# Entry of the feed-forward stage: small weight sums one column tile sooner, weight splits moved in VectorE's queue, output sums and the next splits inside the fixed order

## The chip, the core and the metric

The kernel runs on one core of a Trainium2 chip. A core has five engines with a queue each: TensorE (PE, matmuls; its weight loads are shown as PEld), VectorE (DVE), ScalarE (ACT), GpSimd (POOL), and SyncE (SP), which here only issues transfers. The metric is the device time of one execution in microseconds; lower is better.

## The reference, cut to what matters

The reference is one layer over 1024 tokens of width 1024, all in float32: a normed and modulated mixer (stick-breaking attention beside a gated convolution) with an output projection, and then a feed-forward part. The change lies where the second begins:

```python
x = x + g1 * (merged @ w_out[l])

h = rmsnorm(x, ln2_g[l]) * (1.0 + sc2) + sh2
f = (jax.nn.silu(h @ w_ffn_gate[l]) * (h @ w_ffn_up[l])) @ w_ffn_down[l]
x = x + g2 * f
```

`w_ffn_gate` and `w_ffn_up` have 2816 columns, which are 22 column tiles of 128.

## The kernel before

**Products.** Each float32 operand is cut into a high part (`whi` of a weight, `rh` or `big` of an activation), which ScalarE writes by a copy to a rounded format, and a low part (`wlo`, `rl`), which VectorE writes as the difference (lines 134 and 1031). A product `half_prod` (line 123, called through `prod`) multiplies 512 rows of one 128-column weight tile with 512 tokens: four row tiles, three matmuls each (lines 129, 130, 131: high by high, high by low, low by high), so 12 matmuls of 128x512 into one of eight PSUM banks (`bank()`, line 1018).

**Seven products for a pair of column tiles.** Gate and up are computed for column tile j and column tile j+11 together, from the four 512-row blocks a11, a12, a21, a22 of the two, with seven products instead of eight (a Strassen form). Products 1 and 2 take a11 and a12 as they are; products 6, 5, 7, 3 and 4 take s2, s1, s3, s4 and a22, where s1 to s4 are sums of the blocks that GpSimd makes ("small weight sums", lines 149 to 153 for j = 0, lines 1323 to 1326 later). On the other side stand sums of quarters of the normed activation. Five additions on VectorE then make the four outputs (lines 1299 to 1303 and 1332 to 1342). `strassen(j, e, src)` does this for gate (e = 0) and up (e = 1), eleven times over j.

**The entry.** While the output projection ends (16 products `wo_prod`, a loop over m for token half 0 and one for token half 1), the weights for products 1 and 2 of j = 0 and j = 1 are loaded and split (`pre_weights`), and the raw tiles of j = 0 for the sums are loaded at m = 4 and m = 5. `wo_end` adds the residual on VectorE (line 1069), squares it on ScalarE (1075), stores it, and adds the square to a running sum `acc` on GpSimd (1078); the last square of half 1 is added by VectorE (1181). `sum2` sums over partitions with eight one-column matmuls (1085), `rstd_of` makes the factor (120, 121), and `spread2` brings it to all partitions with eight small matmuls (1091). Then `norm2` (1096) scales the eight tiles of token half 1, and VectorE and ScalarE make the activation factors of products 3, 7, 5, 6 (factor pairs `rh[2]`, `rh[6]`, `rh[5]`, `rh[4]`) and last `rh[3]` for product 4. Between them TensorE runs the products 1 and 2 of gate and up of j = 0 and j = 1 (`pre_prod`), then p3, p7, p6, p5 of gate, q6 of up, p4 of gate, and then q5, q7, q3, q4 of up.

**What sets the order.** From line 1109 to `ends = in_order(i0)` (1285) the order on each engine is the order in which the code is written. `plan_split` allots the buffers of a split and puts it on a list; `split_next` takes the next one from that list and places its ScalarE copy and its VectorE subtraction at this place of the two queues. `whi` and `wlo` are rings of nine buffers each, refilled when TensorE has read them. After line 1285 a planner with a cost model orders the instructions; those of j = 0 on VectorE and ScalarE come behind the last ones of the fixed order (`late`). Buffers of closed pools are used again: a new tile waits for the readers of the tile that lay there. `raw` has four buffers, so each load of a weight tile on SP's queue waits for the split or the sum that last reads an older one. From j = 1 on the sums on GpSimd write the tiles `ws0` to `ws3`, which lie where a quarter of the normed activation (`xb[1][1]`) lay.

In the eight PSUM banks, products 1 and 2 of j = 1 (gate and up) hold four until the loop reaches j = 1. p3, p7 and p5 hold one each until the output additions of gate read them.

Of the kernel before, what the change touches and what calls it, by code (L numbers as in the profile page):

```python
# [8 lines left out]
F32 = mybir.dt.float32  # L9
# [7 lines left out]
P = 128  # L17
# [11 lines left out]
def block_kernel(tc, x, x_t, cols, ada_1, ada_2, ada_row, w_q, w_kv, w_v1, w_cg, w_a, w_b, w_o, w_g, w_u, w_d, out):  # L29
# [1128 lines left out]
    for m in range(KT):  # L1158
# [14 lines left out]
        if m >= 6:  # L1173
            spre.append(sums_in_place(*rsum[m - 6], *((wp.tile([P, 512], F32, name="s2"),) if m == 6 else ())))
# [24 lines left out]
    wq3 = plan_split(s4)  # L1199
# [3 lines left out]
    nc.scalar.activation(ca[0][1], p1, AF.Copy)  # L1203
    p2 = bank()
# [9 lines left out]
    for q in (2, 6, 3):  # L1214
        rh[q] = ep.tile([P, 4, 512], F32R, name=f"rh{q}")
        rl[q] = ep.tile([P, 4, 512], F32R, name=f"rl{q}")
# [4 lines left out]
    wq7 = plan_split(s3)  # L1221
# [18 lines left out]
    split_next()  # L1240
    p3 = bank()
    prod(p3, wq3, 2)
    wq6 = plan_split(s2)
# [8 lines left out]
    for j in range(4):  # L1252
        f_lo(5, j, xs(1, 1, j))
        nc.scalar.activation(rh[4][:, j], xs(0, 0, j), AF.Copy)
# [3 lines left out]
    wq5 = plan_split(s1)  # L1258
# [5 lines left out]
    s1, s2, s3, s4, au22 = spre[1]  # L1264
    s2 = xs(0, 0, 0)
    tt(nc.gpsimd, s2, au22, s3, ALU.subtract)
    tt(nc.gpsimd, s4, s4, s2, ALU.subtract)
    spre[1] = s1, s2, s3, s4, au22
    tt(nc.vector, c21, p6, c21, ALU.add)
    for j in range(4):  # L1270
        tt(nc.vector, xs(1, 0, j), xs(1, 0, j), xs(1, 1, j), ALU.subtract)
        nc.scalar.activation(rh[3][:, j], xs(1, 0, j), AF.Copy)
        if j == 1:
            uq6 = plan_split(s2)
            split_next()
# [6 lines left out]
    tt(nc.vector, ca[1][1], q6, ca[1][1], ALU.add)
    p4 = bank()
    prod(p4, wq4, 3)
    ends = in_order(i0)
    pre[0, 1] = ca[1]
# [284 lines left out]
```

## Time and profile before

| | us |
|---|---|
| median of three runs (lowest, highest) | 1885.09 (1882.09, 1885.92) |
| the profiled execution: its own time | 1887.14 |
| its span, from the first to the last instruction | 1885.0 |
| TensorE busy | 1818.8 (96%) |
| VectorE busy | 1340.6 (71%) |
| ScalarE busy | 777.4 (41%) |
| GpSimd busy | 413.6 (22%) |
| mean granted TensorE clock | 0.987 |

Rows of a timeline give start, duration, engine, line, operation, the tiles written and read, the shape, the count, and in brackets how long the engine had stood idle before, and what ended that. Durations of matmuls that follow each other overlap: a stream at full clock has 0.39 us a matmul, started 0.227 us apart. Rows of the stage view give a stretch, its length, the busy time (and instructions) of PE, PEld, DVE, ACT and POOL, the granted clock as a share of full speed, the transfers' share and rate.

### The profile page before, as it was taken

How to read it: one execution, taken by the hardware profiler on the slowest of the kernel's cores; microseconds unless marked ns; L12 is line 12 of the kernel's file. 1: busy time of each engine (PE TensorE's matmuls, PEld its weight loads, DVE VectorE, ACT ScalarE, POOL GpSimd, SP SyncE). 2: the span in 40 equal slices, each digit the busy share in tenths (PEclk: the TensorE clock that was granted, in tenths of full speed). 3: DMA queues.
4: the chain of work that ended last, by engine and by line, in shares of the span. 5: the costliest groups of instructions: out<-in, count | busy, mean ns of one | idle time of the engine just before them, and what ended most of it. 6: DMA issues, size and time to landing. Idle time of an engine off the chain costs nothing.

```text
span 1885.0 us, 24611 instructions
## 1 busy us (share of the span) xinstructions
PE 1818.8 (96%) x8765; PEld 1506.0 (80%) x8765; DVE 1340.6 (71%) x1896; ACT 777.4 (41%) x1462; POOL 413.6 (22%) x292
## 2 busy tenths in 40 slices
PE   7999999999999999979999999989999999999999
PEld 5787778887788988867888788877888888888787
DVE  6873877779854888867788544579987778743953
ACT  4342653332334656645556322344444344422220
POOL 1043338332420000000000001235554545300000
PEclk9999999999999999989999999998999999999999
DMA  9598452238538566677553534505444344289766
GB/s 389 199 305 302 162 173 79 73 104 303 207 123 254 149 189 180 167 223 219 158 161 101 182 129 167 174 27 169 152 174 155 134 145 169 111 341 320 253 233 214
DMA packets 154112, 351.94 MB, mean 187 GB/s; under 512 B 15211, under 2 KB 54397, under 8 KB 151814
## 3 DMA queue, kind: packets, MB, share of 16 engines
q1 hardware_dynamic: 96336, 239.54, 39.9%
q10 hardware_dynamic: 56646, 107.16, 15.6%
q0 software_dynamic: 1008, 3.67, 0.5%
q8 instruction: 70, 1.15, 0.3%
q14 instruction: 52, 0.43, 0.1%
HBM read 240.73 MB, written 109.58 MB: 186 GB/s over the span
## 4 chain that ended last, share of the span: by engine, by line
PE 78%; DVE 10%; DMA 7%; issue 2%; ACT 2%; POOL 1%; SPq 0%; ACTq 0%; DVEq 0%; POOLq 0%
PE e L129 7%; PE e L130 7%; PE e L131 7%; PE pj L129 5%; PE pj L130 5%; PE pj L131 5%; PE pj L292 5%; PE pj L851 4%; PE pj L852 4%; PE pj L853 4%; PE e L1414 3%; PE e L1412 3%; PE e L1413 3%; PE tr L784 3%; PE o L800 2%
## 5 line engine op out<-in xcount | busy, mean ns | idle before, releaser
L769 DVE TENSOR_TENSOR_SCAN pt<-pt,mk 128x128 f32<-128x128 f32 (+7 forms) x128 | 172.1, 1350 | 54.6 <-ACT pt L765 53.9
L134 POOL TENSOR_TENSOR acc<-acc,sq 128x512 f32<-128x512 f32 x13 | 16.8, 1291 | 650.8 <-ACT sq L1075 650.8
L765 ACT ACTIVATE pt<-z,rq 128x512 f32<-128x512 f32 (+1 forms) x192 | 107.7, 579 | 102.0 <-PE z L764 49.6
L129 PE MATMUL e<-big,whi 128*128 128x512 f32 x352 | 139.6, 396 | 5.5 <-DVE c L134 2.9
L134 DVE TENSOR_TENSOR wlo<-raw,whi 128x512 fp32r<-128x512 f32 x144 | 108.1, 761 | 45.7 <-ACT whi L468 33.5
L134 DVE TENSOR_TENSOR c<-e,c 128x512 f32<-128x512 f32 x154 | 103.2, 682 | 51.4 <-PE e L131 50.2
L130 PE MATMUL e<-big,whi 128*128 128x512 f32 x352 | 139.1, 395 | 0.0
L131 PE MATMUL e<-big,wlo 128*128 128x512 f32 x352 | 139.0, 395 | 0.0
L129 PE MATMUL pj<-big,whi 128*128 128x512 f32 x320 | 125.2, 391 | 5.0 <-ACT whi L468 2.6
L130 PE MATMUL pj<-big,whi 128*128 128x512 f32 x320 | 124.9, 390 | 0.0
L131 PE MATMUL pj<-big,wlo 128*128 128x512 f32 x320 | 124.5, 391 | 0.0
L1412 PE MATMUL e<-f,whi 128*128 128x512 f32 (+1 forms) x319 | 122.1, 383 | 1.3 <-ACT whi L1030 1.3
L1413 PE MATMUL e<-f,whi 128*128 128x512 f32 (+1 forms) x319 | 122.0, 383 | 0.0
L1414 PE MATMUL e<-f,wlo 128*128 128x512 f32 (+1 forms) x319 | 117.2, 384 | 3.3 <-DVE wlo L1031 3.3
L134 DVE TENSOR_TENSOR c<-pj,c 128x512 f32<-128x512 f32 x140 | 92.9, 682 | 34.0 <-PE pj L131 33.7
L134 POOL TENSOR_TENSOR ws<-raw,raw 128x512 f32<-128x512 f32 x40 | 56.9, 1422 | 267.6 <-DMA raw<-w_cg 123.2
L292 PE MATMUL pj<-whi,big 128*128 128x512 f32 x352 | 110.6, 401 | 2.9 <-ACT big L275 2.9
L468 ACT ACTIVATE whi<-raw 128x512 fp32r<-128x512 f32 x116 | 72.4, 628 | 95.4 <-PE pj L130 41.1
L788 DVE TENSOR_TENSOR atl<-tr,ath 128x512 fp32r<-128x512 f32 (+1 forms) x192 | 99.6, 549 | 12.3 <-ACT ath L787 10.7
L787 ACT ACTIVATE ath<-tr 128x512 fp32r<-128x512 f32 (+1 forms) x192 | 86.9, 489 | 48.0 <-PE o L799 29.6
L129 PE MATMUL e<-rh,whi 128*128 128x512 f32 x264 | 103.8, 393 | 2.9 <-DVE c L134 2.9
L851 PE MATMUL pj<-big,whi 128*128 128x512 f32 x256 | 105.0, 410 | 0.0
(255 smaller groups left out, 4992.3 us busy)
## 6 DMA issues: line engine op xcount, KB each, us to landing
f<-d_f SPq DMA_DIRECT2D x77, 512.0 KB, 4.3
d_f<-fs ACTq DMA_DIRECT2D x70, 512.0 KB, 2.7
raw<-w_cg SPq DMA_DIRECT2D x40, 512.0 KB, 3.6
raw<-w_g SPq DMA_DIRECT2D x24, 512.0 KB, 3.4
raw<-w_u SPq DMA_DIRECT2D x24, 512.0 KB, 3.3
ad<-ada ACTq DMA_DIRECT2D x19, 512.0 KB, 4.6
ada<-ada SPq DMA_DIRECT2D x8, 1024.0 KB, 10.3
d_t<-ts SPq DMA_DIRECT2D x16, 512.0 KB, 5.4
```

Of the source, the lines that this page charges most:

```text
L129: nc.tensor.matmul(ps, wh[:, k, :], fh[:, k, :], start=(k == 0), stop=False)
L130: nc.tensor.matmul(ps, wh[:, k, :], fl[:, k, :], start=False, stop=False)
L131: nc.tensor.matmul(ps, wl[:, k, :], fh[:, k, :], start=False, stop=(k == 3))
L134: eng.tensor_tensor(out=out, in0=a, in1=b, op=op)
L292: nc.tensor.matmul(ps, a, b, start=(k == 0 and q == 0), stop=(k == KT - 1 and q == 2))
L765: nc.scalar.activation(pt[:, off + s0:off + s0 + m], z[:, :m], AF.Sigmoid, scale=rq[:, 1, i, h:h + 1])
L769: nc.vector.tensor_tensor_scan(out=pt[:, rev], data0=pt[:, rev], data1=mk[:, rev], initial=1.0, op0=ALU.mult, op1=ALU.max)
L788: nc.vector.tensor_tensor(out=tl[:, :nb, c0:c0 + P], in0=src, in1=th[:, :nb, c0:c0 + P].bitcast(F32), op=ALU.subtract)
L851: nc.tensor.matmul(ps, wh, rh_, start=(k == 0), stop=False)
L1412: nc.tensor.matmul(o, wh, f[:, 0, c], start=(j == 0), stop=False)
L1413: nc.tensor.matmul(o, wh, f[:, 1, c], start=False, stop=False)
L1414: nc.tensor.matmul(o, wl, f[:, 0, c], start=False, stop=(j == NJ - 1))
```

## The change

It moves work in the fixed order. (1) GpSimd makes the sums of the gate's tiles at m = 5 instead of m = 6, and the first two of the up tiles' sums at m = 6 instead of m = 7; the other two (`t2`, and `t4` in place) come before the norm of token half 1 instead of after p5, in a tile of their own (`t2u`) instead of over `xs(0, 0, 0)`. (2) The splits are placed anew: wq7 directly after wq3, wq6 before the first `norm2`, wq5 after the first quarter of `rh[6]`, then uq6 (which fed q6), wq4, and uq5 one place each; uq7 stands among the output sums, uq3 and uq4 behind p4. All of them are in the fixed order; the four of up were the planner's before. (3) Four of the five output additions of gate, and with them the two output tiles `c12` and `c22`, come into the fixed order, ahead of the addition of q6 and of the request for p4's bank. (4) The buffers of `rh[3]`, `rl[3]` are opened after the last use of `t2u`. No operation is added or left out.

```diff
--- before.py
+++ after.py
@@ -1170,8 +1170,10 @@
         if 2 <= m < 6:
             split_next()
             split_next()
-        if m >= 6:
-            spre.append(sums_in_place(*rsum[m - 6], *((wp.tile([P, 512], F32, name="s2"),) if m == 6 else ())))
+        if m == 5:
+            spre.append(sums_in_place(*rsum[0], wp.tile([P, 512], F32, name="s2")))
+        elif m == 6:
+            spre.append(sums_in_place(*rsum[1]))
         ps = wo_prod(m, 1)
         if m == 0:
             r = sum2(0, (acc[0],))
@@ -1196,11 +1198,13 @@
 
     ca = [(ctile(f"c0{e}", cpa), ctile(f"c1{e}", cpa)) for e in range(2)]
     s1, s2, s3, s4, a22 = spre[0]
-    wq3 = plan_split(s4)
+    t1, t2, t3, t4, u22 = spre[1]
+    wq3, wq7 = plan_split(s4), plan_split(s3)
     p1 = pre_prod(0, 0)
     r = sum2(1, (acc[1],))
     split_next()
     nc.scalar.activation(ca[0][1], p1, AF.Copy)
+    split_next()
     p2 = bank()
     half_prod(p2, pw[0][1], rh[1], rl[1], 0, 3)
     rb1 = spread2(r)
@@ -1211,14 +1215,22 @@
     ep = s6.enter_context(tc.tile_pool(name="phe", bufs=1, reuse_waits="tile"))
     th, tl = big(), big()
     rh[4], rh[5], rl[4], rl[5] = th[:, 4:8], th[:, 0:4], tl[:, 4:8], tl[:, 0:4]
-    for q in (2, 6, 3):
-        rh[q] = ep.tile([P, 4, 512], F32R, name=f"rh{q}")
-        rl[q] = ep.tile([P, 4, 512], F32R, name=f"rl{q}")
+
+    def two(q):
+        rh[q], rl[q] = (ep.tile([P, 4, 512], F32R, name=f"r{t_}{q}") for t_ in "hl")
+
+    two(2)
+    two(6)
+    s2u = ExitStack()
+    t2 = s2u.enter_context(tc.tile_pool(name="phs2", bufs=1, reuse_waits="tile")).tile([P, 512], F32, name="t2u")
+    tt(nc.gpsimd, t2, u22, t3, ALU.subtract)
+    tt(nc.gpsimd, t4, t4, t2, ALU.subtract)
 
     def f_lo(q, j, src):
         tt(nc.vector, rl[q][:, j], src, rh[q][:, j].bitcast(F32), ALU.subtract)
 
-    wq7 = plan_split(s3)
+    wq6, wq5, uq6, wq4, uq5, uq7, uq3, uq4 = (plan_split(s) for s in (s2, s1, t2, a22, t1, t3, t4, u22))
+    split_next()
     for j in range(4):
         norm2(j, 1, rb1)
         tt(nc.gpsimd, xs(0, 0, j), xs(0, 1, j), xs(0, 0, j), ALU.subtract)
@@ -1237,10 +1249,10 @@
             op1=ALU.subtract)
         stt(out=xs(0, 1, j), in0=xs(1, 1, j), scalar=dsh2[:, j:j + 1], in1=xs(0, 1, j), op0=ALU.add, op1=ALU.subtract)
         nc.scalar.activation(rh[6][:, j], xs(0, 1, j), AF.Copy)
-    split_next()
+        if j == 0:
+            split_next()
     p3 = bank()
     prod(p3, wq3, 2)
-    wq6 = plan_split(s2)
     for j in range(4):
         stt(out=xs(1, 1, j), in0=xs(1, 1, j), scalar=mod[:, 2, 4 + j:5 + j], in1=xs(0, 0, j), op0=ALU.add,
             op1=ALU.subtract)
@@ -1250,61 +1262,59 @@
     prod(p7, wq7, 6)
     split_next()
     for j in range(4):
+        nc.scalar.activation(rh[4][:, j], xs(0, 0, j), AF.Copy)
         f_lo(5, j, xs(1, 1, j))
-        nc.scalar.activation(rh[4][:, j], xs(0, 0, j), AF.Copy)
     c11, c21 = ca[0]
     p6 = bank()
     prod(p6, wq6, 5)
-    wq5 = plan_split(s1)
     split_next()
     for j in range(4):
         f_lo(4, j, xs(0, 0, j))
     p5 = bank()
     prod(p5, wq5, 4)
-    s1, s2, s3, s4, au22 = spre[1]
-    s2 = xs(0, 0, 0)
-    tt(nc.gpsimd, s2, au22, s3, ALU.subtract)
-    tt(nc.gpsimd, s4, s4, s2, ALU.subtract)
-    spre[1] = s1, s2, s3, s4, au22
+    split_next()
+    s2u.close()
+    ep = s6.enter_context(tc.tile_pool(name="phe3", bufs=1, reuse_waits="tile"))
+    two(3)
     tt(nc.vector, c21, p6, c21, ALU.add)
     for j in range(4):
         tt(nc.vector, xs(1, 0, j), xs(1, 0, j), xs(1, 1, j), ALU.subtract)
         nc.scalar.activation(rh[3][:, j], xs(1, 0, j), AF.Copy)
-        if j == 1:
-            uq6 = plan_split(s2)
-            split_next()
     q6 = bank()
     prod(q6, uq6, 5)
-    wq4 = plan_split(a22)
-    split_next()
     for j in range(4):
         f_lo(3, j, xs(1, 0, j))
+    s5.close()
+    s7 = ExitStack()
+    cp = s7.enter_context(tc.tile_pool(name="phc2", bufs=1, side="right", reuse_waits="tile"))
+
+    def ct(tag, bufs):
+        return cp.tile([P, 512], F32, tag=tag, bufs=bufs, name=nm(tag))
+
+    c12, c22 = ct("c20", 1), ct("c30", 1)
+    tt(nc.vector, c12, p5, c21, ALU.add)
+    split_next()
+    tt(nc.vector, c22, p7, c12, ALU.add)
+    tt(nc.vector, c21, p7, c21, ALU.add)
+    tt(nc.vector, c12, p3, c12, ALU.add)
     tt(nc.vector, ca[1][1], q6, ca[1][1], ALU.add)
     p4 = bank()
     prod(p4, wq4, 3)
+    for _ in range(2):
+        split_next()
+    g00 = c11, c12, c21, c22
     ends = in_order(i0)
     pre[0, 1] = ca[1]
-    s5.close()
-    s7 = ExitStack()
-    cp = s7.enter_context(tc.tile_pool(name="phc2", bufs=1, side="right", reuse_waits="tile"))
-
-    def ct(tag, bufs):
-        return cp.tile([P, 512], F32, tag=tag, bufs=bufs, name=nm(tag))
 
     def strassen(j, e, src):
 
+        if (j, e) == (0, 0):
+            tt(nc.vector, g00[2], p4, g00[2], ALU.add)
+            return g00
         c12, c22 = ct(f"c2{e}", 1), ct(f"c3{e}", 1)
-        if (j, e) == (0, 0):
-            c11, c21 = ca[0]
-            tt(nc.vector, c12, p5, c21, ALU.add)
-            tt(nc.vector, c22, p7, c12, ALU.add)
-            tt(nc.vector, c21, p7, c21, ALU.add)
-            tt(nc.vector, c12, p3, c12, ALU.add)
-            tt(nc.vector, c21, p4, c21, ALU.add)
-            return c11, c12, c21, c22
         if (j, e) == (0, 1):
             c11, c21 = pre[j, e]
-            s1, s2, s3, s4, a22 = spre[1]
+            ws = dict(zip((5, 7, 3, 4), (uq5, uq7, uq3, uq4)))
         else:
             raw = load_raw(src[j])
             a11, a12 = raw[:, :512], raw[:, 512:]
@@ -1327,18 +1337,19 @@
             q6 = bank()
             prod(q6, split(s2), 5)
             tt(nc.vector, c21, q6, c21, ALU.add)
+            ws = {}
         q5 = bank()
-        prod(q5, split(s1), 4)
+        prod(q5, ws.get(5) or split(s1), 4)
         tt(nc.vector, c12, q5, c21, ALU.add)
         q7 = bank()
-        prod(q7, split(s3), 6)
+        prod(q7, ws.get(7) or split(s3), 6)
         tt(nc.vector, c22, q7, c12, ALU.add)
         tt(nc.vector, c21, q7, c21, ALU.add)
         q3 = bank()
-        prod(q3, split(s4), 2)
+        prod(q3, ws.get(3) or split(s4), 2)
         tt(nc.vector, c12, q3, c12, ALU.add)
         q4 = bank()
-        prod(q4, split(a22), 3)
+        prod(q4, ws.get(4) or split(a22), 3)
         tt(nc.vector, c21, q4, c21, ALU.add)
         return c11, c12, c21, c22
```

More of the change, by code (lines that the diff above doesn't have):

```diff
@@ L1272, in block_kernel @@
         nc.scalar.activation(rh[3][:, j], xs(1, 0, j), AF.Copy)
-        if j == 1:
-            uq6 = plan_split(s2)
-            split_next()
     q6 = bank()
     prod(q6, uq6, 5)
-    wq4 = plan_split(a22)
-    split_next()
     for j in range(4):
         f_lo(3, j, xs(1, 0, j))
[L1282 to L1286, printed above, removed]
     s5.close()
@@ L1292, in ct @@
         return cp.tile([P, 512], F32, tag=tag, bufs=bufs, name=nm(tag))
+    c12, c22 = ct("c20", 1), ct("c30", 1)
[4 more added lines that the diff above has]
+    tt(nc.vector, c12, p3, c12, ALU.add)
+    tt(nc.vector, ca[1][1], q6, ca[1][1], ALU.add)
+    p4 = bank()
+    prod(p4, wq4, 3)
+    for _ in range(2):
+        split_next()
+    g00 = c11, c12, c21, c22
+    ends = in_order(i0)
+    pre[0, 1] = ca[1]
     def strassen(j, e, src):
+        if (j, e) == (0, 0):
+            tt(nc.vector, g00[2], p4, g00[2], ALU.add)
+            return g00
         c12, c22 = ct(f"c2{e}", 1), ct(f"c3{e}", 1)
-        if (j, e) == (0, 0):
-            c11, c21 = ca[0]
-            tt(nc.vector, c12, p5, c21, ALU.add)
-            tt(nc.vector, c22, p7, c12, ALU.add)
-            tt(nc.vector, c21, p7, c21, ALU.add)
-            tt(nc.vector, c12, p3, c12, ALU.add)
-            tt(nc.vector, c21, p4, c21, ALU.add)
-            return c11, c12, c21, c22
         if (j, e) == (0, 1):
             c11, c21 = pre[j, e]
-            s1, s2, s3, s4, a22 = spre[1]
+            ws = dict(zip((5, 7, 3, 4), (uq5, uq7, uq3, uq4)))
         else:
```

## The prediction, made blind

> **What bounds the kernel now.** First the page, its chain of waits:
>
> ```profile
> PE 78%; DVE 10%; DMA 7%; issue 2%; ACT 2%; POOL 1%; SPq 0%; ACTq 0%; DVEq 0%; POOLq 0%
> ```
>
> TensorE's matmuls set the end, so a change pays where PE stands idle or runs slowly. Next PE's timeline through the entry, each stall with its neighbours:
>
> ```profile
> 1227.73 0.39 PE L131 MATMUL e<-big,wlo 128*128 128x512 f32 x1
> 1229.78 1.05 PE L1085 MATMUL e<-onec,acc 128*128 128x1 f32 x8 [1.66 <-DVE acc L134]
> ...
> 1233.42 1.91 PE L1091 MATMUL e<-dm,rs_r 128*128 128x128 f32 x8
> ...
> 1263.03 0.39 PE L131 MATMUL e<-big,wlo 128*128 128x512 f32 x1
> 1266.07 0.60 PE L129 MATMUL e<-big,whi 128*128 128x512 f32 x1 [2.65 <-ACT whi L1038]
> ...
> 1273.62 0.76 PE L129 MATMUL e<-rh,whi 128*128 128x512 f32 x1 [2.90 <-DVE c L134]
> ...
> 1280.87 0.76 PE L129 MATMUL e<-big,whi 128*128 128x512 f32 x1 [2.87 <-DVE c L134]
> ...
> 1287.14 0.40 PE L129 MATMUL e<-rh,whi 128*128 128x512 f32 x1
> ```
>
> Stall A (1.66 us) waits for the row sum; B (2.65), C (2.90) and D (2.87) stand before q6, p4 and q5. From 1263.26 (the last matmul of p5 plus 0.227) to 1287.14 PE does 39 matmuls: 12 of q6, 12 of p4, 15 of q5 and q7. At 0.227 each that is 8.84 us; it takes 23.88. So 15.0 are lost, 8.4 of them idle, the rest at a lower clock. Stages of 3.41 us show that:
>
> ```profile
> 1266.29:1269.70 3.41, 3.41 (x9) 2.43 (x9) 2.19 (x4) 2.30 (x4) 0.00 (x0) 0.50 0.00 0
> 1269.70:1273.11 3.41, 1.02 (x5) 0.50 (x3) 3.41 (x7) 3.40 (x7) 0.00 (x0) 0.99 0.45 154
> 1273.11:1276.53 3.42, 2.91 (x7) 2.37 (x8) 3.42 (x3) 0.56 (x2) 3.28 (x3) 0.51 0.00 0
> 1276.53:1279.94 3.41, 1.48 (x6) 0.86 (x5) 3.41 (x3) 1.67 (x3) 2.97 (x2) 1.00 0.16 26
> 1279.94:1283.35 3.41, 2.48 (x6) 2.02 (x7) 3.41 (x7) 1.56 (x3) 0.00 (x0) 0.51 0.87 237
> 1283.35:1286.77 3.42, 3.42 (x9) 2.65 (x9) 3.42 (x7) 1.37 (x3) 0.00 (x0) 0.50 0.96 296
> ```
>
> The clock, third number from the end, is about 1 or about 0.5 and changes at these cuts: after a stage in which PE was busy 2.91 us or more it is full, after 2.48 or less it is half. A stall is paid twice.
>
> Why PE waits stands in VectorE's timeline:
>
> ```profile
> 1227.99 1.73 DVE L134 TENSOR_TENSOR acc<-acc,sq 128x512 f32<-128x512 f32 x1 [1.80 <-POOL acc L134]
> ...
> 1235.36 1.41 DVE L1096 SCALAR_TENSOR_TENSOR xb<-xb,a,e 128x512 f32<-128x512 f32 x2 [3.72 <-PE e L1091]
> ...
> 1261.97 2.86 DVE L134 TENSOR_TENSOR xb<-xb,xb 128x512 f32<-128x512 f32 x2
> 1266.05 0.69 DVE L134 TENSOR_TENSOR wlo<-xb,whi 128x512 fp32r<-128x512 f32 x1 [1.22 <-ACT whi L1038]
> ...
> 1269.17 0.69 DVE L134 TENSOR_TENSOR wlo<-raw,whi 128x512 fp32r<-128x512 f32 x1 [1.22 <-ACT whi L1038]
> 1269.78 2.49 DVE L134 TENSOR_TENSOR rl<-xb,rh 128x512 fp32r<-128x512 f32 x4
> ...
> 1272.79 0.68 DVE L134 TENSOR_TENSOR c<-e,c 128x512 f32<-128x512 f32 x1
> 1273.39 6.74 DVE L1031 TENSOR_TENSOR wlo<-raw,whi 128x512 fp32r<-128x512 f32 x4
> 1280.05 0.68 DVE L134 TENSOR_TENSOR c<-e,c 128x512 f32<-128x512 f32 x1
> ```
>
> From the first norm2 (1235.36) on, VectorE is the pace-maker. p4 and q5 wait for PSUM banks: four are held by the products of j = 1, three by p3, p7 and p5, so one passes from p6 to q6 to p4. C ends with the addition of q6 (1272.79 + 0.68), D with the first output addition (1280.05 + 0.68). That one is late because the four splits before it took 6.74 us, where four like operations took 2.49. GpSimd's timeline says why:
>
> ```profile
> 1259.80 2.81 POOL L134 TENSOR_TENSOR xb<-raw,raw 128x512 f32<-128x512 f32 x1 [18.54 <-DVE big L134]
> ...
> 1273.25 1.28 POOL L134 TENSOR_TENSOR ws<-raw,raw 128x512 f32<-128x512 f32 x1 [8.96 <-DMA raw<-w_g]
> ...
> 1276.17 3.41 POOL L134 TENSOR_TENSOR ws<-raw,ws 128x512 f32<-128x512 f32 x2
> ```
>
> While its sums run, VectorE's operations with two SBUF inputs take about 1.67 us instead of 0.60; the pair at 1261.97 was hit by the sums from 1259.80 on. An addition with a PSUM input (1280.05) keeps 0.68.
>
> **The change, part by part.** I count from E, the end of the spread (1233.42 + 1.91 = 1235.33), to R, the 39th matmul (1287.14), behind which PE streams.
>
> *Sums a tile sooner: E moves by 0.3.* The stall goes only if the last addition to acc comes before 1227.96.
>
> ```profile
> 1211.21 1.29 POOL L134 TENSOR_TENSOR acc<-acc,sq 128x512 f32<-128x512 f32 x1 [3.29 <-ACT sq L1075]
> 1220.63 1.74 POOL L134 TENSOR_TENSOR raw<-raw,raw 128x512 f32<-128x512 f32 x1
> ...
> 1210.79 7.42 SPq L1023 DMA_DIRECT2D raw<-w_u  x2
> ...
> DMA to landing us min/median/max: 3.2/4.9/5.9
> ```
>
> The gate sums start at about 1212.5 instead of 1220.63. There they run beside the splits of the last early weights; each two-input operation of VectorE there waits for a sum in progress, I estimate 2.2 us in all (two sums of 1.28, less overlap). The second up load waits in SP's queue for just that split (issued 1218.2, the end of SP's row), as does the residual's load behind it. It would leave at 1220.4. The up sums move ahead of m = 6's addition to acc, and wait for this load: with 4 to 4.9 us to land (the last row, of the raw loads from 1180 to 1300; its median is 4.9), two sums and the addition at 1.28 end at 1228.3 to 1229.2, VectorE's addition 0.7 later, at 1229.0 to 1229.9, against 1229.72 before. Bounds: 0.6 worse, if it lands later still; 2.4 better, if 0.9 of the stall goes and with it the half clock on the spread (0.95 of its 1.91) and three matmuls (0.2 each). I take 0.3, the middle of those two ends.
>
> *wq6 before norm2: 3.2 lost.* Here the change adds a wait. The ring has nine buffers; wq3 and wq7 fill two, the eight early weights the rest, so wq6 takes the buffer of the second early product, which three matmuls after the spread still read: 2 x 0.227 + 0.39 = 0.85 after E. ScalarE's copy follows (0.61, by the wait at 1255.35 below), then VectorE's subtraction. Behind them stand ScalarE's eviction of the next product and rh2, and all eight norm2 on VectorE. GpSimd meanwhile makes t2 and t4, 1.28 each from E on, since t2u lies where the closed pool's row factors lay, which the spread reads (by tile sizes, 32 KB in both pools ahead). The subtraction comes at E + 1.5, inside the second sum, starts at E + 2.65 and ends at E + 3.2. Before, norm2 began at E. Bounds: 0, if another buffer is free; 2.0, if it slips in between the sums. PE's cover is six early products, 6 x 2.72 = 16.3 us.
>
> *Norm2 to the first remainder of rh3: 5.1 gained.* Before: 1269.78 - 1235.36 = 34.4.
>
> ```profile
> 1241.77 0.69 DVE L134 TENSOR_TENSOR c<-e,c 128x512 f32<-128x512 f32 x1 [0.45 <-PE e L131]
> ...
> 1248.98 0.69 DVE L134 TENSOR_TENSOR wlo<-raw,whi 128x512 fp32r<-128x512 f32 x1 [1.22 <-ACT whi L1038]
> ...
> 1255.35 0.69 DVE L134 TENSOR_TENSOR wlo<-s,whi 128x512 fp32r<-128x512 f32 x1 [0.61 <-ACT whi L1038]
> ```
>
> Gone: one split of five (0.60), the 0.45, the two waits of 1.22 at 1266.05 and 1269.17, and GpSimd's hold on the pair at 1261.97 (2.86 - 1.21 = 1.65). Staying: 1.22 (now wq5 inside the loop waits for ScalarE's rh6) and 0.61 (now uq6). That leaves 29.3. Stall B goes with it.
>
> *First remainder of rh3 to p4: 3.7 lost.* Before 1273.62 - 1269.78 = 3.84. p4 now takes the bank that the first output addition frees, directly behind the four remainders. But the gate sums of j = 1 now fall on these: their last raw tile is freed by wq4's split, about 6 us earlier, so the transfer has landed, and what holds them is the tile xb[1][1], free with the last subtraction before the remainders. Price: the row at 1273.39, four at 6.66, and 0.82 from the addition's start to PE (1280.05 to 1280.87): 7.5. Bounds: 3.25 without the sums (2.41 + 0.68 + 0.14); 10.5 if p4 gets q6's bank again, five operations of 0.60 later.
>
> *p4 to R: 5.2 gained.* Before 1287.14 - 1273.62 = 13.52. q5 finds its bank free (1.8 us after the first output addition, while p4 runs), so D is gone: 27 matmuls, 6.1 us. The clock: PE has idled over 3.4 us, so it starts at half and stays so to the end of the first stage that is busy enough, 2.7 to 6.0 us, half of it lost. I take 2.2; 8.3 in all. [...]
>
> *At nothing:* rh3's buffers wait for uq6's split, some 7 us earlier on the same queue; c12 and c22 lie over xb[0][0], last read four operations before; ScalarE and VectorE in the rh4 loop only change places in the text. uq3 and uq4 stand behind the last addition q5 needs. The next up loads leave at about 1279 as before (their buffers are freed by uq3 and uq4). Without these covers each costs one wait of 0.6 to 1.2.
>
> *Sum:* 0.3 - 3.2 + 5.1 - 3.7 + 5.2 = 3.7 gained. Behind R the rows say PE has no idle to give and VectorE some slack:
>
> ```profile
> 1300.00:1338.00 38.00, 38.00 (x170) 31.46 (x169) 35.52 (x43) 18.71 (x34) 21.17 (x14) 1.00 0.54 194
> 1338.00:1376.00 38.00, 38.00 (x169) 31.48 (x168) 36.23 (x45) 17.59 (x30) 21.25 (x14) 1.00 0.48 182
> ...
> 1282.45 1.28 DVE L1031 TENSOR_TENSOR wlo<-ws,whi 128x512 fp32r<-128x512 f32 x2
> ...
> 1294.65 0.39 PE L129 MATMUL e<-big,whi 128*128 128x512 f32 x1
> ```
>
> The first split of j = 1 leads its product by 12.2 us, so the gain is kept. The profiled execution, 1887.14 us (span 1885.0), would become 1883.4; it stands 2.05 above the median, which would become 1885.09 - 3.7 = 1881.4.
>
> **Rivals.** (a) *The port stays free*: GpSimd's sums miss the remainders, or wq6 slips through, or stall A goes. 4.2 more (7.5 to 3.25): 1877.2; with 1.2 and 2.1 from the others 1873.9. For it: the sums were held by a transfer before (8.96). Against: that now leaves some 10 us sooner.
> (b) *The bank comes late*: p4 waits for the addition of q6 as now, 3.0 later: 1884.4. That the fixed order then does nothing for D's bank speaks for it; against it, that banks so far went out in the order in which they came free.
> (c) *Slower: VectorE becomes the bound in j = 1 and 2.* It is busy 35.5 and 36.2 of 38 us while PE does not wait; the planner orders everything behind R anew. Where one split or addition per tile comes after PE, PE waits and loses clock, as at C: 2.9 + 1.5. Two such places: 1881.4 + 8.8 = 1890.2. It decides when the lead of 12.2 is used up; I see 2 to 3 of it go.
>
> **How the numbers follow.** Forecast 0.50, own range 1878.5 to 1884 (gain 1 to 6.5); (a) 0.20; (b) 0.13; (c) 0.17. The time is the forecast's, 1881.4. The range goes from the far end of (a), 1873.5, to (c), 1890. A measurement of this kernel tells about 0.2%, 3.8 us, from no change, and the forecast stands at that bound: of its 0.50 I count 0.30 as faster. Faster 0.30 + 0.20 = 0.50, same 0.20 + 0.13 = 0.33, slower 0.17.
>
> **What would show it.** Right: stall A still over 1 us; norm2 starting 2 to 3 us after the spread, behind a wlo; no wait before q5; one wait of some 7 us before p4, ended by VectorE's c, with four rl of about 1.67 each and ws on GpSimd beside them; half clock after it. Wrong: rl at 0.60 (a), p4 released by the addition of q6 (b), PE idle between 1290 and 1380 (c), or a first norm2 directly behind the spread.

## The result, and the profile after

The changed kernel takes 1874.85 us (median of 4 runs, 1874.54 to 1876.13), the kernel before beside it 1885.51 us (1882.09 to 1886.05, 4 runs): ratio 0.9949, 95% interval 0.9931 to 0.9966. A second series gave 0.9958 (0.9945 to 0.9972; 1877.86 us over 12 runs against 1885.78 us over 35). One of those 35 took 2557.76 us at a granted clock of 0.657, and the ratio leaves it out. Both intervals lie below 1: the changed kernel is faster, by 8 to 11 us (0.4 to 0.6%) where 3.7 us were forecast. The profiled execution took 1874.59 us, its span 1872.5 (before 1887.14 and 1885.0); mean granted clock 0.991 (0.987).

TensorE's timeline through the entry, cut to the ends of stretches; the bracket gives the idle time ahead and what ended it:

```profile
1227.77 0.39 PE L131 MATMUL e<-big,wlo 128*128 128x512 f32 x1
1229.04 1.05 PE L1085 MATMUL e<-onec,acc 128*128 128x1 f32 x8 [0.88 <-DVE acc L134]
...
1232.13 1.05 PE L1091 MATMUL e<-dm,rs_r 128*128 128x128 f32 x8
...
1261.89 0.50 PE L129 MATMUL e<-big,whi 128*128 128x512 f32 x1 [0.24 <-DVE c L134]
...
1267.40 0.47 PE L129 MATMUL e<-rh,whi 128*128 128x512 f32 x1 [2.48 <-DVE c L134]
...
1271.28 0.50 PE L129 MATMUL e<-big,whi 128*128 128x512 f32 x1 [0.90 <-DVE c L134]
...
1274.85 0.39 PE L129 MATMUL e<-rh,whi 128*128 128x512 f32 x1
```

Stall A is 0.88 us (before 1.66), the wait before q6 0.24 (2.65), before p4 2.48 (2.90), before q5 0.90 (2.87). R, the matmul that stood at 1287.14, stands at 1274.85. VectorE and GpSimd beside it:

```profile
1228.29 0.69 DVE L134 TENSOR_TENSOR acc<-acc,sq 128x512 f32<-128x512 f32 x1 [0.83 <-ACT sq L1075]
...
1234.35 0.82 DVE L134 TENSOR_TENSOR wlo<-s,whi 128x512 fp32r<-128x512 f32 x1 [2.84 <-ACT whi L1038]
1235.10 1.40 DVE L1096 SCALAR_TENSOR_TENSOR xb<-xb,a,e 128x512 f32<-128x512 f32 x2
...
1264.16 2.50 DVE L134 TENSOR_TENSOR rl<-xb,rh 128x512 fp32r<-128x512 f32 x4
1266.56 0.69 DVE L134 TENSOR_TENSOR c<-e,c 128x512 f32<-128x512 f32 x1
```

```profile
1233.34 1.29 POOL L134 TENSOR_TENSOR t2u<-raw,raw 128x512 f32<-128x512 f32 x1 [1.55 <-PE e L1091]
1234.70 1.62 POOL L134 TENSOR_TENSOR raw<-raw,t2u 128x512 f32<-128x512 f32 x1
...
1264.38 3.40 POOL L134 TENSOR_TENSOR ws<-raw,raw 128x512 f32<-128x512 f32 x1 [23.04 <-ACT rh L1282]
```

The four remainders (`rl`) take 2.50 us, although GpSimd's first sum for j = 1 comes 0.22 us after the start of the first of them. It is the sum that waits: 1.28 us of work take 3.40, and its end, 1267.78, lies 1.12 us behind the end of VectorE's last remainder (1266.66), about one sum's length. Two stages around the wait before p4, and two long ones behind R:

```profile
1263.15:1266.57 3.42, 1.77 (x8) 1.13 (x6) 3.42 (x7) 3.40 (x8) 2.19 (x1) 1.00 0.00 0
1266.57:1269.98 3.41, 2.58 (x11) 2.18 (x12) 3.29 (x5) 1.83 (x2) 3.41 (x3) 1.00 0.02 5
...
1300.00:1338.00 38.00, 38.00 (x169) 31.48 (x168) 36.76 (x48) 17.95 (x32) 17.35 (x12) 1.00 0.50 184
1338.00:1376.00 38.00, 38.00 (x169) 31.46 (x169) 36.15 (x46) 18.18 (x33) 19.13 (x13) 1.00 0.49 178
```

The clock stays full through the wait before p4, and behind R PE is busy all the time, as before.

Two marks make runs comparable, since the time at which the entry begins differs by up to 9 us between the profiles: S, the start of the last matmul ahead of the row sum (1227.73 before, 1227.77 after), and R. E is the end of the spread. All in us, from one profile each:

| kernel | S to E | E to R | R to end of span | S to end |
|---|---|---|---|---|
| before | 7.60 | 51.81 | 597.86 | 657.27 |
| before, second profile | 6.21 | 50.55 | 598.70 | 655.46 |
| changed | 5.41 | 41.67 | 597.65 | 644.73 |
| changed, second profile | 5.57 | 41.80 | 597.75 | 645.12 |

So the gain is made between S and R, 12.3 us in the first pair and 9.4 in the second, and nothing of it is lost behind.

### The profile page after: what moved, and what is told of

The parts are those of the page before. It is cut to its first block, busy times and chain, and to the rows that moved or that the text cites. A ratio compares the mean times of both kernels' runs of the same rounds, so it can differ in the third digit from the quotient of the medians.

```text
span 1872.5 us, 24605 instructions
## 1 busy us (share of the span) xinstructions
PE 1813.7 (97%) x8765; PEld 1503.2 (80%) x8765; DVE 1343.1 (72%) x1896; ACT 777.7 (42%) x1462; POOL 415.5 (22%) x292
## 4 chain that ended last, share of the span: by engine, by line
PE 76%; DVE 11%; DMA 6%; issue 3%; ACT 2%; POOL 1%; SPq 0%; ACTq 0%; DVEq 0%; POOLq 0%
PE e L129 6%; PE e L130 6%; PE e L131 6%; PE pj L129 5%; PE pj L292 5%; PE pj L130 5%; PE pj L131 5%; PE pj L851 4%; PE pj L852 4%; PE pj L853 4%; PE e L1425 3%; PE e L1423 3%; PE e L1424 3%; PE tr L784 3%; PE o L800 2%
## 5 line engine op out<-in xcount | busy, mean ns | idle before, releaser
L134 DVE TENSOR_TENSOR wlo<-raw,whi 128x512 fp32r<-128x512 f32 x148 | 114.1, 782 | 43.3 <-ACT whi L468 32.4
L129 PE MATMUL e<-big,whi 128*128 128x512 f32 x352 | 137.6, 391 | 1.2 <-DVE c L134 1.1
L130 PE MATMUL e<-big,whi 128*128 128x512 f32 x352 | 137.3, 390 | 0.0
L129 PE MATMUL pj<-big,whi 128*128 128x512 f32 x320 | 125.9, 393 | 4.2 <-ACT whi L468 2.7
L130 PE MATMUL pj<-big,whi 128*128 128x512 f32 x320 | 125.5, 392 | 0.0
L784 PE MATMUL tr<-dm,pt 128*128 128x128 f32 x576 | 97.0, 278 | 10.6 <-DVE atl L788 10.3
```

The lines of the kernel that those rows point to most:

```text
L129: nc.tensor.matmul(ps, wh[:, k, :], fh[:, k, :], start=(k == 0), stop=False)
L130: nc.tensor.matmul(ps, wh[:, k, :], fl[:, k, :], start=False, stop=False)
L134: eng.tensor_tensor(out=out, in0=a, in1=b, op=op)
L784: nc.tensor.transpose(tr[:, j * P:(j + 1) * P], pt[:, off + (b0 + j) * P:off + (b0 + j + 1) * P], ident)
```

## The experiments

**The changed kernel again** (no edit).

> The changed kernel unaltered, timed beside the three variants. 1874.9 us is its median so far; the run is the base for the others. Nothing is told apart by it alone, except how far its profile repeats: if the full clock after the 2.48 us wait before p4 was an accident of where the 3.41 us stages of the clock fell, this profile may show half clock there (p4 to R 1 to 2 us longer, a run near 1876.5); if a wait of 2.48 us never costs clock, it will not.

It shows half clock behind the wait before p4. Two stages of it, cut where its clock changes:

```profile
1267.41:1270.82 3.41, 1.48 (x7) 0.90 (x5) 3.41 (x7) 3.39 (x7) 2.47 (x1) 1.00 0.00 0
1270.82:1274.24 3.42, 2.87 (x7) 2.32 (x8) 3.30 (x4) 1.77 (x3) 3.42 (x3) 0.50 0.02 5
```

The wait is 2.48 us in both profiles. Here one stage holds 1.93 of it, PE is busy 1.48 of 3.41, and the next stage runs at half; in the first profile the cut at 1266.57 divides it, PE is busy 1.77, and the clock stays. In the first profile the changes of clock fall on one grid (those at 24.11 and 911.58 us are 260 steps of 3.413 apart), so where it cuts a wait is an accident of the execution. The price was small: p4 to R 7.58 against 7.45, since the wait before q5 was gone. The slow p4 used up the time that PE would have waited. The next two versions and the first one without gaps were timed in this series, so their times go against 1877.86.

**Sums late.** The sums of j = 0 stand in lines 1149 to 1153 of the kernel before. The edit:

```diff
-        if m == 5:
-            spre.append(sums_in_place(*rsum[0], wp.tile(...)))
-        elif m == 6:
-            spre.append(sums_in_place(*rsum[1]))
+        if m >= 6:
+            spre.append(sums_in_place(*rsum[m - 6], ...))
```

> The changed kernel with the sums of the raw weight tiles put back to m = 6 and m = 7; all else stays. Theory (the gain is a sum of separate pieces, the earlier end of the spread one of them with 2.15 us): stall A returns with 1.6 to 1.7 us, the spread and the matmuls beside it run at half clock, E comes 2.1 to 2.2 later, and all behind it with it: 1877.0, between the two kernels. Rival 1 (the whole gain hangs on the sums sooner): 1885. Rival 2 (the early products of PE cover it, so that E is of no account): 1874.9.

Measured: 1877.51 us, ratio to before 0.9963 (0.9952 to 0.9975); S to E 6.21, E to R 41.63. Stall A is back (1.69), the half clock is not. So the sums themselves are worth 0.6 to 0.8; the other 1.4 of the 2.19 between S and E was half clock on the spread and the matmuls just ahead of it in the first profile of before (S to E 7.60; clock 0.50 from 1232.18 to 1235.60), absent in its second one (6.21; 1.00 from 1231.94 to 1238.77). The 2.1 to 2.5 us by which S to end grows (647.26) come mostly from behind R (599.42), where the edit does nothing and a stretch of half clock shows near 1765 (the mean granted clock from 1765 to 1770 is 0.68; in the changed kernel it is 1.00). The times of the two are not to be told apart.

**Output additions of gate back to the planner.** The edit:

```diff
-    tt(nc.vector, c12, p5, c21, ALU.add)
-    split_next()
-    tt(nc.vector, c22, p7, c12, ALU.add)
-    tt(nc.vector, c21, p7, c21, ALU.add)
-    tt(nc.vector, c12, p3, c12, ALU.add)
     tt(nc.vector, ca[1][1], q6, ca[1][1], ALU.add)
     p4 = bank()
     prod(p4, wq4, 3)
-    for _ in range(2):
+    for _ in range(3):
         split_next()
```

> The changed kernel with the four output additions of gate given back to the planner, as before; the three splits of up then stand directly behind the addition of q6. Theory (the fixed order of the additions removes the wait before q5): p4 starts where it does now, since the addition of q6 stands in the place of the first output addition; then three splits alternate with GpSimd's sums at about 1.7 us each, the first output addition ends 4 to 5 us after p4's start, PE waits 2.0 to 2.6 us before q5 in place of 0.90, and may lose up to 1.7 to the half clock behind it: 1.4 to 3.1 slower, 1876.3 to 1878.0. Rival 1 (the additions carry the whole p4-to-R gain of 6.07): 1880.9. Rival 2 (the splits' places alone did it): 1874.9.

Measured: 1877.02 us, 0.9952 (0.9939 to 0.9966); E to R 42.72, 1.0 more, S to end 644.77. The three splits took 4.54 us. p4 ran at half clock (0.50 from 1269.65 to 1273.05), so that only 0.63 of the late addition showed as a wait before q5 (2.0 to 2.6 were expected). A fixed order of the additions is worth about 1 us at R, and nothing that the whole time shows.

**The addition of p6 behind the subtractions.** The edit, in the changed kernel:

```diff
-    tt(nc.vector, c21, p6, c21, ALU.add)
     for j in range(4):
         tt(nc.vector, xs(1, 0, j), xs(1, 0, j), xs(1, 1, j), ALU.subtract)
         nc.scalar.activation(rh[3][:, j], xs(1, 0, j), AF.Copy)
+    tt(nc.vector, c21, p6, c21, ALU.add)
```

> The changed kernel with one move: the addition of p6, whose input is in PSUM, stands behind the four subtractions for rh3 and not ahead of them, so that it lies directly between them and the four remainders. Theory (who holds the port when the other comes decides: VectorE's unbroken run keeps GpSimd out, GpSimd in first makes both alternate): GpSimd's first sum starts during this addition, then the four remainders take 6.5 to 6.7 us and not 2.50, p4 starts 7 to 8 us after the first of them (now 3.24), PE waits 5 to 6 us, with half clock behind it; from the last matmul ahead of the row sum to R 50 to 52 us, against 46.9 now. Rival (the sums lost the race because VectorE has the right of way, always): remainders at 2.50 again, 47.0.

VectorE, then GpSimd and PE of this run:

```profile
1264.88 0.68 DVE L134 TENSOR_TENSOR c<-e,c 128x512 f32<-128x512 f32 x1
1265.48 6.49 DVE L134 TENSOR_TENSOR rl<-xb,rh 128x512 fp32r<-128x512 f32 x4
```

```profile
1265.10 1.28 POOL L134 TENSOR_TENSOR ws<-raw,raw 128x512 f32<-128x512 f32 x1 [22.43 <-ACT rh L1281]
1266.34 1.74 POOL L134 TENSOR_TENSOR ws<-raw 128x512 f32<-128x512 f32 x1
1268.04 3.38 POOL L134 TENSOR_TENSOR ws<-raw,ws 128x512 f32<-128x512 f32 x2
```

```profile
1273.32 0.77 PE L129 MATMUL e<-rh,whi 128*128 128x512 f32 x1 [4.67 <-ACT fs L1360]
```

The addition reads PSUM; GpSimd's sum starts beside it, undelayed (1.28), and from then on the two alternate: 6.49 us for four remainders, p4 7.84 after the first of them (0.60 of it another operation of VectorE, which the planner put ahead of the first output addition), E to R 47.17. (The wait before p4 is put down to ScalarE; it ended 0.15 us after VectorE's first output addition.) One operation in another place, and the forecast's own term is there. This run and the three others that were timed only once (1882.59 us here, splits to the planner 1884.11, sums alone 1881.01, the kernel before again 1891.08) are read by their profiles alone.

**Splits of up back to the planner.** The edit:

```diff
-    wq6, wq5, uq6, wq4, uq5, uq7, uq3, uq4 = (plan_split(s) for s in (s2, s1, t2, a22, t1, t3, t4, u22))
+    wq6, wq5, uq6, wq4 = (plan_split(s) for s in (s2, s1, t2, a22))
...
-            ws = dict(zip((5, 7, 3, 4), (uq5, uq7, uq3, uq4)))
+            s1, s3, s4, a22, ws = t1, t3, t4, u22, {}
```

with the four `split_next()` of these left out.

> The changed kernel with the four splits of up (uq5, uq7, uq3, uq4) given back to the planner, while the output additions stay in the fixed order. Theory (the splits in VectorE's idle places shorten the queue ahead of p4, by 0.60 each, and their places ahead of the additions made the old wait before q5): one split less ahead of p4, so p4 0.6 sooner; the planner puts the splits behind the additions, alternating with GpSimd's sums; q5 needs the first of them, wq5 of up, and PE waits for it 2 to 4 us in place of 0.90; 48 to 50 us to R. Rival (the order of the additions alone removed the old wait): 46.5.

More time is lost, as expected (43.1 us from E to R, 1.5 more than in the changed kernel), but at another place: PE waits 4.07 us before p4 and not at all before q5. The planner put a product of ScalarE's result (`c<-c,c`, 1.44 us beside a sum) ahead of the first output addition, so p4's bank came late. The splits in the fixed order keep that place free; that is an observation of one profile.

**The earlier sums alone**, in the kernel before (the edit of the sums above, reversed).

> The kernel before with the earlier sums alone. Theory: stall A falls from 1.66 to 0.9 to 1.1 us, the row sum starts 0.6 to 0.8 sooner; everything behind the spread stays as before (first norm2 directly behind it, stalls of 2.65, 2.90 and 2.87 before q6, p4 and q5), so E to R is again 51 to 52 us. From the last matmul ahead of the row sum to R: 57 to 58.5, against 59.18 before. Rival (the sums carry the gain): 47 to 50.

Theory and rival were both wrong for the way to R. Stall A is 1.07 us, as expected, and S to E 7.16 (with half clock on the matmuls ahead of the spread, 0.50 from 1230.0 to 1233.4), but E to R is 46.33, 5.5 less than in the first profile of before and 4.2 less than in the second, and the wait before q5 is gone. VectorE and GpSimd show why:

```profile
1271.39 0.68 DVE L134 TENSOR_TENSOR c<-e,c 128x512 f32<-128x512 f32 x1
1271.99 0.68 DVE L134 TENSOR_TENSOR c<-c,c 128x512 f32<-128x512 f32 x1
1272.59 2.49 DVE L1031 TENSOR_TENSOR wlo<-raw,whi 128x512 fp32r<-128x512 f32 x4
```

```profile
1272.59 3.63 POOL L134 TENSOR_TENSOR ws<-raw,raw 128x512 f32<-128x512 f32 x1 [9.09 <-DMA raw<-w_g]
```

The planner had put the operation with two SBUF inputs (`c<-c,c`) between the addition of q6 and the four splits. GpSimd came while VectorE was in a run of such operations and had to wait; the splits took 2.49 us and not 6.74. So stall D of the kernel before was this race, lost. (The place of `c<-c,c` in the planner's order, which differs between the two, goes with it; the edit did not name that place.)

**The kernel before, profiled again** (no edit).

> The kernel before, profiled a second time. Theory (the race for the port is decided by the moment at which GpSimd's first sum comes, and that sum is released by a transfer): if the load of raw lands while the addition of q6 runs, as in the first profile, the four splits take 6.7 us again and q5 waits 2.9; if it lands outside, the splits take 2.5, the wait before q5 is under 1 us or gone, and from the matmul ahead of the row sum to R it is 4 to 6 us less than 59.18. Stalls A, B and C as in the first profile, within 0.3 us each; where half clock follows one, it depends on where the stages of 3.41 us fall. Rival (the order of the queues alone fixes it): 58.5 to 59.5 again.

```profile
1277.05 0.68 DVE L134 TENSOR_TENSOR c<-e,c 128x512 f32<-128x512 f32 x1
1277.65 6.79 DVE L1031 TENSOR_TENSOR wlo<-raw,whi 128x512 fp32r<-128x512 f32 x4
```

```profile
1277.58 1.27 POOL L134 TENSOR_TENSOR ws<-raw,raw 128x512 f32<-128x512 f32 x1 [9.04 <-DMA raw<-w_g]
```

Lost again: GpSimd's sum starts during the addition of q6, 0.07 us ahead of the first split (0.14 in the first profile). The waits before p4 and q5 are 4.26 and 1.86, together 6.12 (5.77 in the first profile). The one before p4 was expected within 0.3 of 2.90; it is longer here, where q6 ran at full clock (0.50 only from 1276.36 on) and not, as there, at half (0.50 from 1266.29 to 1269.70). That the landing of the load turns it in other executions was not seen.

**Versions without the gaps.** The remaining waits of the changed kernel come from VectorE's queue between E and p4. The first version takes three delays out of it and moves the addition of p6 as above:

```diff
-    split_next()
     for j in range(4):
         norm2(j, 1, rb1)
...
         nc.scalar.activation(rh[2][:, j], xs(1, 1, j), ...)
+    split_hi()
+    split_hi()
...
-        if j == 0:
-            split_next()
+        if j == 1:
+            split_lo()
+            split_hi()
+        if j == 2:
+            split_lo()
...
     prod(p7, wq7, 6)
-    split_next()
+    split_lo()
```

(`split_hi` places ScalarE's copy of a split, `split_lo` VectorE's subtraction.)

> The changed kernel with wq6's split behind the norm, its ScalarE copy and those of wq5 and uq6 placed where ScalarE is idle, some us ahead of VectorE's subtractions, and the addition of p6 behind the four subtractions for rh3. Theory (from the spread to p4 VectorE's queue sets PE's pace): E to first norm2 falls from 1.92 to about 0.03, the waits of 1.22 and 0.62 for ScalarE's copies go, so p4's bank comes 3 to 4 us sooner than PE can use it; of the 0.24 + 2.48 + 0.90 us that PE waits there, 3 to 3.6 go: 1871.5. Rival 1 (a wait for a bank or for ScalarE's copies takes their place): 1874.9. Rival 2 (what PE gains here it gives back behind R, where VectorE has 2 us of slack in 38): 1874.9, with new waits of PE for wlo after 1290.

1879.21 us, 0.9971 (0.9959 to 0.9983): no gain. The first norm does follow the spread directly, but the four remainders took 6.49 us, for the reason of the run above, and PE waited 4.69 us before p4. The next version keeps VectorE's run whole:

```diff
+    c12 = spre[0][1]
     for j in range(4):
         tt(nc.vector, xs(1, 0, j), xs(1, 0, j), xs(1, 1, j), ALU.subtract)
         nc.scalar.activation(rh[3][:, j], xs(1, 0, j), AF.Copy)
+        if j == 0:
+            tt(nc.vector, c21, p6, c21, ALU.add)
+        if j == 2:
+            tt(nc.vector, c12, p5, c21, ALU.add)
-    tt(nc.vector, c21, p6, c21, ALU.add)
...
-    c12, c22 = ct("c20", 1), ct("c30", 1)
-    tt(nc.vector, c12, p5, c21, ALU.add)
-    split_next()
+    c22 = ct("c30", 1)
     tt(nc.vector, c22, p7, c12, ALU.add)
     tt(nc.vector, c21, p7, c21, ALU.add)
+    split_next()
```

> The run without gaps once more, with VectorE's run ahead of p4 kept whole: the addition of p6 stands behind the first of the four subtractions and the first output addition (in the tile of s2) behind the third, so that from the fourth subtraction to the last remainder no operation with a PSUM input gives GpSimd the port. Theory: remainders at 2.5 us, p4's bank free before PE has done q6, no wait or one under 0.6 us before p4 and q5; the spread to R in 37 to 38 us (now 41.4), and with the row sum as now 42.5 to 43.5 from the matmul ahead of it; 3.5 to 4.5 us faster than the changed kernel's 1877.9 beside e4, if the chip is as then. Rival 1 (the port is taken all the same): remainders at 6.5, 47 or more. Rival 2 (PE gives it back behind R): as e8 up to R, and then waits of PE between 1280 and 1380.

Up to R it did what it should: remainders 2.49, no wait of PE at all before q6, p4 and q5, E to R 36.95. Behind R it gave the gain back:

```profile
1297.70 0.50 PE L129 MATMUL e<-big,whi 128*128 128x512 f32 x1 [3.78 <-DVE c L134]
```

R to the end 601.89 (changed kernel 597.65), S to end 645.95, 1876.51 us, 0.9963 (0.995 to 0.9976). The 26 us from R on, and what VectorE and GpSimd waited for there:

```profile
1272.51:1298.51 26.00, 22.22 (x98) 17.87 (x97) 22.14 (x26) 8.65 (x16) 15.95 (x11) 1.00 0.45 145
```

```profile
1286.76 1.23 DVE L1031 TENSOR_TENSOR wlo<-ws,whi 128x512 fp32r<-128x512 f32 x1 [3.86 <-ACT whi L1030]
```

```profile
1281.23 2.22 POOL L134 TENSOR_TENSOR ws<-raw 128x512 f32<-128x512 f32 x1 [7.29 <-DVE c L134]
```

VectorE (third pair of numbers) is not full in this version: it is busy 22.14 of 26 us and stands 3.86 us for ScalarE's copies of GpSimd's sums. Those sums begin 45.7 us after E, as in the changed kernel (1278.90), although R comes 4.7 us sooner after E. Behind them VectorE's operations alternate with the next sums, at some 1.75 us each, and the addition that frees PE's bank comes last. Two versions tried VectorE's load there, by giving it GpSimd's sums (all twelve, or the four output sums of j = 0):

```diff
-        feng = nc.vector if j == NJ - 1 else nc.gpsimd
+        feng = nc.vector if j in (0, NJ - 1) else nc.gpsimd
...
-            tt(nc.gpsimd, s3, a11, a21, ALU.subtract)
...
+            seng = nc.vector if j == 1 else nc.gpsimd
+            tt(seng, s3, a11, a21, ALU.subtract)
...
```

> The version of e8 with GpSimd's work of the tight stretch given to VectorE: the eight sums of raw tiles for j = 1, and the four sums of outputs for j = 0; nothing else. A sum on GpSimd that alternates with VectorE costs VectorE 1.07 us (1.67 in place of 0.60), one on VectorE 0.60. Theory: up to R as e8 (the spread to R in 36 to 37.5 us); the 3.8 us wait near 1298 falls under 1.5, since the twelve operations add 7.2 us to VectorE's queue and up to 12.8 go from it; from R to the end 598 to 599.5, against 602.12 in e8; 1873 to 1874.5 beside a kernel before of 1883 to 1885. Rival (VectorE is full, and 7.2 us more make it later): a longer wait near 1298, 604 or more from R to the end.

> As e10, with only the four sums of outputs for j = 0 on VectorE; the eight sums of raw tiles stay on GpSimd. Two of the four fall ahead of the wait near 1298, so VectorE gains 2 x (1.07 - 0.60) = 0.9 us there: the wait 2.5 to 3.2 in place of 3.8, R to the end 601 to 601.8. Rival (the sums on GpSimd are not what makes VectorE late): no change against e8, 602.1.

1875.65 us, 0.9954 (0.9938 to 0.997), and 1876.05 us, 0.9955 (0.9939 to 0.9971). The waits fell to 3.03 and 1.97, with half clock behind each (matmuls started 0.43 us apart), which the wait of 3.78 did not have (0.23). R to the end is 602.11 and 602.77, so both theories failed. With twelve sums the rival failed too (it expected a longer wait and 604 or more); with four its time was nearer. The last version is to free two PSUM banks of j = 1 some 20 us sooner:

```diff
-        c12, c22 = ct(f"c2{e}", 1), ct(f"c3{e}", 1)
+        c12 = ct(f"c2{e}", 1) if e else spre[0][1]
+        c22 = ct(f"c3{e}", 1)
...
-            c11, c21 = (ctile(f"c{q}{e}", cpa) for q in range(2))
+            c11 = ctile(f"c0{e}", cpa)
+            c21 = ct("c20", 1) if (j, e) == (1, 1) else ctile(f"c1{e}", cpa)
```

> The version of e11 with a tile of its own for the third output of up of j = 1 (the first output addition of gate always goes to s2, so one tile is spare). In e11 the wait near 1295 ended with the addition that frees the bank of up's product 2 of j = 1; it stood behind ScalarE's copy into a tile that j = 0 still held until 1287, and then behind eight contended operations of VectorE. With the spare tile the copy and the addition go ahead before R, and both banks of up come free some 20 us sooner. Theory (after the gaps ahead of R are gone, PSUM banks held for j = 1 are what PE meets next): no wait of PE between R and 1400, R to the end 597.9 to 598.8, R as in e11 or 0.6 later (the addition now stands in the queue ahead of R): 640.5 to 641.5 from the matmul ahead of the row sum to the end, against 644.7 and 645.1 in the changed kernel, and a median 3 to 4 us below the changed kernel's. Rival (VectorE's work as a whole is the bound there): a wait of 1 us or more comes at the next bank, and 601 or more from R to the end.

1876.31 us, 0.9954 (0.9938 to 0.9969). The theory failed and the rival held: the wait moved to the next bank and half clock follows it (0.50 from 1300.9 to 1304.3), R to the end is 601.05, and PE waits 0.88 us before q5. The 26 us from R on, in the changed kernel and here:

```profile
1274.85:1300.85 26.00, 25.91 (x114) 21.14 (x113) 23.40 (x26) 8.37 (x15) 19.00 (x12) 1.00 0.55 198
```

```profile
1274.75:1300.75 26.00, 23.96 (x106) 19.52 (x104) 25.85 (x31) 9.20 (x17) 13.01 (x9) 1.00 0.55 172
...
1300.91 0.80 PE L129 MATMUL e<-big,whi 128*128 128x512 f32 x1 [2.20 <-ACT c L1347]
```

VectorE is busy 23.40 of 26 us in the changed kernel and 25.85 here (26.00 with all twelve sums). With GpSimd's sums on it, it has no slack left. In the version that left them on GpSimd it had, and PE waited too. So what PE wins ahead of R beyond the changed kernel it waits for behind R in all four; whether VectorE's work or the coming of the sums is the bound there, these runs do not settle. None of these versions is faster than the changed kernel by what the series tell apart.

| run | S to E | E to R | R to end of span | S to end |
|---|---|---|---|---|
| sums late | 6.21 | 41.63 | 599.42 | 647.26 |
| additions to the planner | 5.52 | 42.72 | 596.53 | 644.77 |
| p6 behind | 5.41 | 47.17 | 598.82 | 651.40 |
| splits to the planner | 5.57 | 43.14 | 598.38 | 647.09 |
| sums alone | 7.16 | 46.33 | 598.15 | 651.64 |
| no gaps | 5.45 | 44.38 | 597.81 | 647.64 |
| no gaps, run kept | 7.11 | 36.95 | 601.89 | 645.95 |
| twelve sums on VectorE | 5.56 | 37.06 | 602.11 | 644.73 |
| four sums on VectorE | 5.49 | 36.96 | 602.77 | 645.22 |
| banks early | 7.05 | 37.76 | 601.05 | 645.86 |

In the profile of the splits to the planner the matmuls around R carry mixed names; R is counted there in order of time.

## Why the prediction was right, and where it was wrong

The sign was right and the time lay in the whole range (1873.5 to 1890), but outside the forecast's own 1878.5 to 1884: the size was that of rival (a) with its two additions (1873.9), to which 0.20 was given. Term by term, between the two profiles (gains positive):

| term | forecast | measured |
|---|---|---|
| sums a tile sooner (E) | 0.3 | 2.15 |
| wq6 before norm2 | -3.2 | -1.89 |
| norm2 to first remainder of rh3 | 5.1 | 5.36 |
| first remainder of rh3 to p4 | -3.7 | 0.60 |
| p4 to R | 5.2 | 6.07 |
| sum | 3.7 | 12.29 |

*First remainder to p4* is the step that failed: 3.7 us lost were forecast, 0.60 were gained. Its premise held: the transfer had landed, and the sum came 0.14 us after the last subtraction (row end 1264.24), though the bracket of its row names ScalarE. Its price did not: I took the row of 6.74 us for what happens whenever GpSimd's sums and VectorE's operations meet, and that row is one of two cases. With VectorE's run already going and unbroken (changed kernel, sums alone, no gaps with the run kept), four operations take 2.5 us and GpSimd waits for the end of the run. With GpSimd in first, through an operation that reads PSUM (before, p6 behind, no gaps), they take 6.5 to 6.8. The run with p6 behind the subtractions shows the forecast's case with its forecast price (7.84 for 7.5). A row that I quoted held the other case, GpSimd waiting: GpSimd's sum at 1259.80 took 2.81 us and not 1.28, because VectorE's run went on to 1261.46. I read from it only what it did to the pair behind it.

*Sums a tile sooner*: the second up load left at 1220.07 (forecast 1220.4), and the transfer landed early enough (its sum starts 3.5 us later, where 4 to 4.9 were reckoned): GpSimd's last addition to acc ended ahead of ScalarE's last square, which VectorE now waits for (0.83). Stall A stayed, at 0.88 in the first profile and 1.05 in the second (over 1 us was the sign). The 2.15 is near the bound of 2.4, but 1.4 of it was half clock in one profile of before and not in the other; what the edit itself gives is 0.6 to 0.8.

*wq6 before norm2*: the wait is there, E to the first norm2 1.92, by the bound that I gave as 2.0: the subtraction slipped in between t2 and t4 (1234.63). *Norm2 to the first remainder* was right to 0.3: the waits of 1.22 and 0.62 that it kept are there, and those that it struck are gone. It is the second largest term, and it is read from the two profiles: no run gives it back by itself.

*p4 to R*: right in size, wrong in both parts, so the size was luck. A wait before q5 stayed (0.90), and no clock was lost (2.2 forecast), since the wait before p4 was 2.48 us and not 7; in the second profile half clock came and took the place of the wait before q5. That D goes was put down to the order of the additions; the sums alone, which leave the additions to the planner, lose D too, by winning the race. In the kernel before, D was the price of the race.

*Clock reading*: a stage that is busy 2.48 us or less is followed by half clock, I wrote. That 2.48 was of a stage already at half. From full clock, 1.77 and 1.86 (sums late) were followed by full, and 1.02 (in the prediction) by half. At 1.48 both occur. It was half in the second profile of the changed kernel (and behind the row at 1276.53 in the prediction); with the splits given to the planner, and in the run kept whole (1292.44 to 1295.86), the clock stayed full. The first of these:

```profile
1270.42:1273.83 3.41, 1.48 (x7) 0.90 (x5) 3.18 (x7) 3.38 (x6) 2.56 (x1) 1.00 0.00 0
1273.83:1277.24 3.41, 1.27 (x6) 1.09 (x7) 3.38 (x5) 3.12 (x6) 3.41 (x3) 1.00 0.00 0
```

A stage that holds the eight one-column matmuls of the row sum (1.05 us) does not fit the order either: in the first profile of before, 2.40 us of busy time with them were followed by half clock. So PE's busy time in a stage does not decide alone; what else does stays open. A stage 43% busy (1.48 of 3.41 us) was followed by half clock in two profiles, and by full clock in two others.

Rival (b) did not come. Rival (c) did not come in the changed kernel, where PE stays busy behind R. The later versions without gaps, whose R comes some 4 us sooner still, ran into waits of its kind at the place that it names: in j = 1, 2 to 3.8 us long, with half clock behind three of the four. VectorE was full in the three that gave it GpSimd's sums, not in the first.

## What to carry to other kernels

Where GpSimd and VectorE both work on SBUF, look at what VectorE does at the moment when GpSimd's operation is released. A run of VectorE without an operation that reads PSUM keeps its pace here (four operations in 2.50 us, changed kernel), and one such operation in front of the run cost 4 us (6.49, p6 behind); so place PSUM additions at the head of a run only where no GpSimd work is waiting. Price a collision by both kinds of rows that the profile has, those where VectorE is slow and those where GpSimd is, and ask which case the new order makes. A stall that a profile shows once may be a race or a cut of the clock's grid: profile the kernel before twice before a gain is put down to an edit.

## What the runs showed of the hardware

In these profiles VectorE (in operations with two SBUF inputs) and GpSimd delayed each other, and the one that met the other at work took longer: four operations of VectorE took 6.74 us behind a sum (before) and 2.49 without one, a sum of 1.28 us took 3.40 behind a run of VectorE (changed kernel). An operation of VectorE that reads PSUM kept its 0.68 us beside a sum (p6 behind, 1264.88). Behind that, the two are not alike: a run of VectorE's operations with SBUF inputs let GpSimd wait through up to four of them (sums of 1.28 us took 3.40 and 3.63), while GpSimd's sums, also issued one behind the other, let a waiting VectorE operation in after each (6.49 us for four; in the first profile of before the four end 0.54 to 0.56 us behind the ends of four sums). Why a run goes on, when in the alternating case the second VectorE operation waits again, the runs do not show, nor what it is that the two share: "port" in the prediction and the expectations is a name for it.

Half clock behind a wait of 2.48 us came in one profile of the changed kernel, where the grid left PE busy 1.48 of a stage's 3.41 us, and not in the other, where it left 1.77, and it cost 0.13 us at R where another wait stood behind it. A wait of 3.78 us cost no clock at all where the grid divided it (no gaps, run kept: PE busy 1.48 and 1.57 of 3.41 us in its two stages).
